# Retention heads on one Trainium2 core: read out at the products, scale later, and pair the rotary columns by partition

## The chip, the cores and the metric

The kernel runs on one core of a Trainium2 chip. The time is device microseconds of one execution. Before the change the median of three runs is 1224.99 us (1224.96 to 1226.88). The engines are named as in the profile: PE (TensorE matmul) with PEld (its weight load), DVE (VectorE), ACT (ScalarE), POOL (GpSimd) and SP (the queue that issues most of the DMAs).

## What is computed

Two layers run over a context of 256 tokens and a latent stream of 256 tokens, 1024 wide: first retention with four heads, then a recurrent block, each followed by a gated convolutional feed-forward block. The change lies in the retention layer. Cut to what matters:

```python
q, k, v, g = split(h @ w_in)               # 4 heads; q, k: 256 wide, v, g: 512 wide per head
q, k = rope_2d(q), rope_2d(k * 256**-0.5)  # latent tokens only
y = retention(q, k, v)                     # scores * decay, times v, both directions
out = (silu(g) * groupnorm(y) * gn) @ w_out
# rot inside rope_2d, once by row and once by column of the token grid:
#   x1, x2 = halves;  [x1*cos - x2*sin, x1*sin + x2*cos]
```

The mean in groupnorm is taken out of v beforehand, so that the norm of a head is one factor per token: the reciprocal root of the mean square over the head's 512 channels.

## The kernel before, in words

Channels lie on the partitions, tokens (256 of context, then 256 latent) on the free axis. The weights arrive as 128x128 blocks, eight to a unit of 128x1024, in the order of use that `make_plan` (L96) writes down; 16 blocks make a piece. Each unit is split into a rounded high part `whi` (a copy, on ACT here) and a rest `wlo` (a DVE subtraction, L452), and each activation likewise into `hi` (ACT, L544) and `lo` (DVE, L545). One 128x128 block of a product is therefore three matmuls, high by high, high by low and low by high, L522 to L524 in `mm3`. The third needs `wlo`. `blk` (L506) calls `prep_units` whenever a unit is entered: with a look-ahead of two it issues the `whi` of the unit three ahead on ACT and the `wlo` of the unit two ahead on DVE.

Every engine works through its queue in program order. Side work is put into those queues by `tick` (L357), called once after most products: it issues up to four pending adaLN products, each a multiplication on ACT (L579, `adap`) and an addition on POOL (L580, `ada`); a step of splitting the recurrent block's weights ahead (L471 on ACT, L479 on DVE, results stored by DMA from ACT's queue, `kept`); and up to n deferred functions. `flush` issues all that is deferred.

The loop over heads in `retention` (L1115) runs for head h, where a "product" of q, k or a gate is one unit of weights, 24 matmuls of 512 columns:

- q0, q1, k0, k1: the four column blocks of q and k. Block q0 holds the 128 channels turned by the token's row, 64 x1 above 64 x2, q1 those turned by its column. After each, `tick(2)` and `rope_split` (L893): the context half is split at once, the latent half is turned with `ra` = x cos (L903) and `rb`, built of two operations of 64 partitions each since x1 and x2 are swapped between the halves (L904, L905), then added (L907), and its split is deferred.
- for heads 1 and 2 then the output product of the head before (`ret_out`, four units of weights), and the first gate g0; for head 3 only g0.
- `ret_scores` (three groups of scores times the decay), `ret_v` (four units), gate g1, `ret_av` (weights by v: four PSUM banks `av`, their squares added up on DVE, L992), gate g2, the decay factors of the next head, `ret_stats` (L995: one matmul, a square root on ACT and a reciprocal on DVE, `rstd`, L679), gate g3, and `ret_z` (L1000).

`ret_z` defers five steps. Step c computes `zt` = `av` * gn * `rstd` (L1007, one operand in PSUM), then `zt` * `sg` with the gate's SiLU (L1008, both operands in SBUF), and splits the `zt` of the step before. These steps come out in the ticks of the next head's q and k products, and the four `av` banks stay taken until then. Head 0 has its q, k and two gates from `start`, and its `ret_stats` and `ret_z` are called within head 1, after q0. Head 2's output product is left to the end, after head 3's gates.

Of the kernel before, what the change touches and what calls it, by code (L numbers as in the profile page):

```python
# [8 lines left out]
F32R = mybir.dt.float32r  # L9
AF = mybir.ActivationFunctionType  # L10
ALU = mybir.AluOpType

P = 128
D = 1024
KD = D // P
NT = 512
NS = 256
# [23 lines left out]

CST = {}
NCST = 0
for _n, _w in (("ident", 128), ("sel", 24), ("cos", 512), ("sin", 512), ("dist", 384), ("dpos", 384),
               ("dneg", 384)):
    CST[_n] = (NCST, _w)
    NCST += _w
# [9 lines left out]
def qk_cols(h):  # L57
    return [2 * h, 2 * h + 1, 8 + 2 * h, 8 + 2 * h + 1]
# [37 lines left out]
def make_plan():  # L96
# [4 lines left out]
    def mat(name, ks, cs, kouter=False):  # L101
        ks, cs = list(ks), list(cs)
        blocks.extend((name, k, c) for k in ks for c in cs) if kouter else \
            blocks.extend((name, k, c) for c in cs for k in ks)
# [16 lines left out]
    for h in range(HEADS):  # L121
        if h == 0:
            mat("ret_in", range(KD), qk_cols(0) + [32, 33], True)
            mat("ret_in", range(KD), [34])
        else:
            mat("ret_in", range(KD), qk_cols(h))
            if h < 3:
                out(h - 1)
            mat("ret_in", range(KD), [32 + 4 * h])
        mat("ret_in", range(KD), range(16 + 4 * h, 20 + 4 * h), True)  # L130
        mat("ret_in", range(KD), range(32 + 4 * h + (3 if h == 0 else 1), 36 + 4 * h))
    out(2)
# [164 lines left out]
class Net:  # L297
# [592 lines left out]
                                    self.cc("ident"), ALU.add)  # L890
        self.dd = dd

    def rope_split(self, ps, c):  # L893

        nc = self.nc
        hi = self.slot(dt=F32R, name="qkhi")
        lo = self.slot(dt=F32R, name="qklo")
        a = self.slot([P, NS], name="ra")
        b = self.slot([P, NS], name="rb")
        cos = self.cc("cos", c * NS, NS)  # L900
        sin = self.cc("sin", c * NS, NS)
        nc.scalar.copy(hi[:, :NS], ps[:, :NS])
        nc.vector.tensor_tensor(a, ps[:, NS:], cos, ALU.mult)  # L903
        nc.vector.tensor_tensor(b[0:64], ps[64:128, NS:], sin[64:128], ALU.mult)  # L904
        nc.vector.tensor_tensor(b[64:128], ps[0:64, NS:], sin[0:64], ALU.mult)  # L905
        nc.vector.tensor_tensor(lo[:, :NS], ps[:, :NS], hi[:, :NS].bitcast(F32), ALU.subtract)
        nc.vector.tensor_tensor(a, a, b, ALU.add)  # L907
        self.defer(lambda: self.split(a, hi[:, NS:], lo[:, NS:]))
        return hi, lo

    def ret_scores(self):
        nc = self.nc
# [60 lines left out]
        self.nc.scalar.activation(t, ps, AF.Silu)  # L973
        self.sg.append(t)

    def ret_av(self):
        nc = self.nc
        self.sync()
        self.av, self.avsg = [], self.sg
        acc = None  # L980
        for c in range(4):
            ps = self.ps(name="av")
            for j in range(4):
                self.mm3(ps if j < 2 else ps[:, NS:], [t[:, c * P:(c + 1) * P] for t in self.vs[j]], self.pr[j],
                         j == 0, j == 3)
            self.av.append(ps)
            sq = self.slot(name="gsq")
            nc.scalar.activation(sq, ps, AF.Square)
            if acc is None:
                acc = sq  # L990
            else:
                nc.vector.tensor_tensor(acc, acc, sq, ALU.add)  # L992
        self.gacc = acc

    def ret_stats(self):  # L995
        ps = self.ps(name="gst")
# [3 lines left out]
    def ret_z(self, h):  # L1000

        nc = self.nc
        zs, av, sg, rs = [], self.av, self.avsg, self.grs

        def first(c):
            t = self.slot(name="zt")
            nc.vector.scalar_tensor_tensor(t, av[c], self.pc("gn", 4 * h + c), rs, ALU.mult, ALU.mult)  # L1007
            nc.vector.tensor_tensor(t, t, sg[c], ALU.mult)  # L1008
            hi = self.slot(dt=F32R, name="zhi")
            lo = self.slot(dt=F32R, name="zlo")  # L1010
            return t, hi, lo

        def step(c):
            if c:
                t, hi, lo = prev.pop()
                self.split(t, hi, lo)
                zs.append((hi, lo))
            if c < 4:
                prev.append(first(c))

        prev = []
        self.defer(*[lambda c=c: step(c) for c in range(5)])
        return zs

# [90 lines left out]
    def retention(self):  # L1115
# [5 lines left out]
        zs = None  # L1121
        for h in range(HEADS):
            self.sg = []
            if h == 0:
                qk = [self.rope_split(pss[j], j % 2) for j in range(4)]
                self.silu_g(pss[4])
                self.silu_g(pss[5])
                self.ret_g(h, hl, 2)
                self.decay(0)
            else:  # L1130
                qk = []
                for j, c in enumerate(qk_cols(h)):
                    ps = self.gemm("ret_in", range(KD), c, lambda k: [(0, hl[k])], NT)
                    if h == 1 and j == 0:
                        self.ret_stats()
                        zs = self.ret_z(0)
                    self.tick(2)
                    qk.append(self.rope_split(ps, j % 2))
                self.flush()
                if h < 3:  # L1140
                    self.ret_out(h - 1, zs)
                else:
                    zprev = zs
                self.ret_g(h, hl, 0)
            self.qk = (qk[:2], qk[2:])
            if h == 0:
                self.ret_v(h, hl)
                self.flush()
                self.ret_scores()
                self.ret_g(h, hl, 3)  # L1150
                self.ret_av()
                self.decay(1)
            else:
                self.flush()
                self.ret_scores()
                self.ret_v(h, hl)
                self.ret_g(h, hl, 1)
                self.ret_av()
                self.ret_g(h, hl, 2)
                if h < 3:  # L1160
                    self.decay(h + 1)
            if h:
                self.ret_stats()
                self.ret_g(h, hl, 3)
                zs = self.ret_z(h)
        self.ret_out(2, zprev)
        self.flush()
        self.need("f0")
# [493 lines left out]
def shape_constants():  # L1662
# [7 lines left out]
    def put(name, a):  # L1670
        o, w = CST[name]
        cst[:, o:o + w] = a

    cos, sin = [], []
    for pos in (t // GRID_W, t % GRID_W):
        ang = freqs[:, None] * pos.astype(np.float32)[None, :]
        cos.append(np.concatenate([np.cos(ang), np.cos(ang)], 0))
        sin.append(np.concatenate([np.sin(ang), -np.sin(ang)], 0))
    put("cos", np.concatenate(cos, 1))
    put("sin", np.concatenate(sin, 1))  # L1680
    dist = np.arange(384)[None, :] - 128.0 - np.arange(P)[:, None]
    put("dist", dist)
    put("dpos", np.maximum(dist, 0))
# [9 lines left out]
def pack(inputs):  # L1693
# [7 lines left out]
    for l in range(2):  # L1701
        mats[f"up{l}"] = a["ffn_w_up"][l]
        mats[f"down{l}"] = a["ffn_w_down"][l]
    order = np.array(lru_order())
    both = np.concatenate([order, W + order])
    mats["lru_in"] = mats["lru_in"][:, both]
# [84 lines left out]
```

## Time and profile before

| What | Before |
|---|---|
| median of three runs | 1224.99 us |
| the profiled execution's own time | 1223.15 us |
| its span, first to last instruction | 1221.4 us |
| PE busy | 1186.3 us (97%) |
| DVE busy | 892.5 us (73%) |
| ACT busy | 731.9 us (60%) |
| POOL busy | 360.0 us (29%) |
| mean granted PE clock | 0.988 |

The profiled execution took 1.8 us less than the median of the three runs, and its span leaves out 1.75 us around the first and last instruction. A share of busy time is an average over stages: where PE is busy 97% of the span, the rest lies in few places, and they are found with the list of PE's waits and the timeline. [...]

### The profile page before, as it was taken

To read this page: it belongs to the slowest core of one execution; us is meant where nothing else is said; L and a number is where in the kernel's file an instruction comes from. 1 tells how busy PE (TensorE), PEld (TensorE's weight loads), DVE (VectorE), ACT (ScalarE), POOL (GpSimd) and SP (SyncE) were. 2 spreads that over 40 slices of the span, in tenths; PEclk is the share of its full clock that TensorE was granted. 3 is DMA by queue.
4 is the path that set the end of the run, shared out by engine and by line. 5 is a ranking of instruction groups with operands and counts; after the bars stand their busy time and mean duration, and the time that the engine had idled before them with its cause. 6 is when DMAs were issued, how large, how long until landed. Compare 5 with 4: busy or idle time off the path is not lost.

```text
span 1221.4 us, 18028 instructions
## 1 busy us (share of the span) xinstructions
PE 1186.3 (97%) x6768; PEld 1010.2 (83%) x6768; DVE 892.5 (73%) x1285; ACT 731.9 (60%) x1100; POOL 360.0 (29%) x238
## 2 busy tenths in 40 slices
PE   9999799999979999999999999999999999999997
PEld 5678688778868889877878888789988788999996
DVE  5665996896596598599945676754658877988743
ACT  5465566765753545987643656542497956666542
POOL 0000555746370012798733435360000001000010
PEclk9999899999989999999999999999999999999999
DMA  9975479758566482445688645654586994655631
GB/s 334 339 253 216 182 238 318 250 193 310 208 224 212 145 319 100 143 154 191 215 313 268 222 153 203 231 196 159 162 313 204 327 333 162 193 187 183 195 107 35
DMA packets 79160, 265.38 MB, mean 217 GB/s; under 512 B 9312, under 2 KB 13024, under 8 KB 79072
## 3 DMA queue, kind: packets, MB, share of 16 engines
q1 hardware_dynamic: 66976, 221.75, 54.0%
q10 hardware_dynamic: 12096, 42.47, 8.9%
q8 instruction: 53, 0.87, 0.3%
q14 instruction: 35, 0.29, 0.1%
HBM read 219.62 MB, written 42.99 MB: 215 GB/s over the span
## 4 chain that ended last, share of the span: by engine, by line
PE 78%; DVE 12%; ACT 3%; DMA 3%; issue 2%; SPq 1%; DVEq 0%; ACTq 0%
PE ps L522 22%; PE ps L524 22%; PE ps L523 22%; DVE wlo L452 3%; PE ps L946 2%; PE ps L947 2%; PE ps L948 2%; DVE rstd L679 1%; ACT adap L579 1%; DVE fzlo L545 1%; PE av L524 1%; PE av L523 1%; PE av L522 1%; DVE zt L1007 1%; PE ps L1639 1%
## 5 line engine op out<-in xcount | busy, mean ns | idle before, releaser
L580 POOL TENSOR_TENSOR ada<-ada,adap 128x512 f32<-128x512 f32 x196 | 324.2, 1679 | 365.5 <-ACT adap L579 232.4
L524 PE MATMUL ps<-hhi,wlo 128*128 128x512 f32 (+1 forms) x640 | 245.6, 384 | 11.2 <-DVE wlo L452 11.2
L522 PE MATMUL ps<-hhi,whi 128*128 128x512 f32 (+1 forms) x640 | 248.7, 389 | 0.0
L523 PE MATMUL ps<-hlo,whi 128*128 128x512 f32 (+1 forms) x640 | 244.2, 382 | 0.0
L665 POOL TENSOR_TENSOR sq<-sq,sq 128x256 f32<-128x256 f32 x29 | 32.4, 1127 | 472.9 <-ACT sq L659 382.9
L523 PE MATMUL ps<-hx,whi 128*128 128x256 f32 x592 | 168.1, 284 | 0.4 <-DVE hx L698 0.2
L522 PE MATMUL ps<-hx,whi 128*128 128x256 f32 x592 | 168.3, 284 | 0.2 <-ACT hx L697 0.2
L524 PE MATMUL ps<-hx,wlo 128*128 128x256 f32 x592 | 167.5, 283 | 0.0
L524 PEld LDWEIGHTS ps<-hhi,wlo 128*128 128x128 f32 x640 | 121.6, 190 | 37.4 <-DVE wlo L452 14.5
L522 PEld LDWEIGHTS ps<-hhi,whi 128*128 128x128 f32 x640 | 121.7, 190 | 31.6 <-issue 6.5
L523 PEld LDWEIGHTS ps<-hlo,whi 128*128 128x128 f32 x640 | 121.7, 190 | 22.9 <-issue 1.0
L522 PEld LDWEIGHTS ps<-hx,whi 128*128 128x128 f32 x592 | 113.5, 192 | 4.2 <-issue 2.5
L523 PEld LDWEIGHTS ps<-hx,whi 128*128 128x128 f32 x592 | 113.5, 192 | 1.2 <-DVE hx L698 0.8
L524 PEld LDWEIGHTS ps<-hx,wlo 128*128 128x128 f32 x592 | 113.5, 192 | 0.0
L1190 DVE SCALAR_TENSOR_TENSOR cv<-ps,par,cv 128x510 f32<-128x510 f32 (+1 forms) x88 | 53.9, 613 | 61.7 <-ACT cv L1187 61.7
L1187 ACT ACTIVATE cv<-ps,par 128x512 f32<-128x512 f32 (+1 forms) x88 | 58.7, 670 | 65.8 <-PE ps L524 64.9
L522 PE MATMUL ps<-fzhi,whi 128*128 128x512 f32 (+1 forms) x198 | 72.7, 367 | 0.0
L524 PE MATMUL ps<-fzhi,wlo 128*128 128x512 f32 (+1 forms) x198 | 72.4, 365 | 0.0
L523 PE MATMUL ps<-fzlo,whi 128*128 128x512 f32 (+1 forms) x198 | 72.4, 365 | 0.0
L708 DVE SCALAR_TENSOR_TENSOR xc<-ps,mod,xc 128x256 f32<-128x256 f32 x48 | 23.0, 479 | 54.5 <-PE ps L524 54.4
L524 PE MATMUL ps<-zhi,wlo 128*128 128x512 f32 (+1 forms) x152 | 55.7, 366 | 7.4 <-DVE wlo L452 7.4
L1191 DVE SCALAR_TENSOR_TENSOR cv<-ps,par,cv 128x510 f32<-128x510 f32 (+1 forms) x88 | 54.2, 616 | 3.1
(791 smaller groups left out, 2786.4 us busy)
## 6 DMA issues: line engine op xcount, KB each, us to landing
kept<-pre ACTq DMA_DIRECT2D x40, 512.0 KB, 5.7
whi<-kept SPq DMA_DIRECT2D x40, 512.0 KB, 4.3
wlo<-kept SPq DMA_DIRECT2D x40, 512.0 KB, 5.5
ak<-wpk SPq DMA_DIRECT2D x32, 256.0 KB, 6.3
xc<-xt SPq DMA_DIRECT2D x4, 256.0 KB, 3.7
x<-xt SPq DMA_DIRECT2D x4, 256.0 KB, 5.2
xst<-xhi SPq DMA_DIRECT2D x16, 64.0 KB, 3.8
cst<-cst SPq DMA_DIRECT2D x3, 192.0 KB, 5.1
```

Of the source, the lines that this page charges most:

```text
L452: self.eng(e).tensor_tensor(d[q, o:n], r[q, o:n], hi[q, o:n].bitcast(F32), ALU.subtract)
L522: mm(ps, w[0], x[0], start=start, stop=False)
L523: mm(ps, w[0], x[1], start=False, stop=False)
L524: mm(ps, w[1], x[0], start=False, stop=stop)
L580: nc.gpsimd.tensor_tensor(acc[i, s], acc[i, s], t, ALU.add)
L665: nc.gpsimd.tensor_tensor(self.acc[s], self.acc[s], sq, ALU.add)
L946: mm(pss[t], xh, wh, start=k == 0, stop=False)
L947: mm(pss[t], xh, wl, start=False, stop=False)
L948: mm(pss[t], xl, wh, start=False, stop=k == KD - 1)
L1187: nc.scalar.activation(acc, ps[:, :n], AF.Identity, scale=w(1), bias=self.pc("fcb", layer * 44 + f))
L1190: nc.vector.scalar_tensor_tensor(a3[:, :, 1:], p3[:, :, :NS - 1], w(0), a3[:, :, 1:], ALU.mult, ALU.add)
L1191: nc.vector.scalar_tensor_tensor(a3[:, :, :NS - 1], p3[:, :, 1:], w(2), a3[:, :, :NS - 1], ALU.mult, ALU.add)
```

## The change

Four edits go together.

1. `rope_split`: the columns of q and k are laid out anew when the weights are packed, so that a block holds all x1 (rows' 64, then columns' 64) and the next block their partners x2. Turning a pair takes a cosine product and a sine product of 128 partitions for each block, and then one subtraction and one addition. Both splits are deferred after the second block. The cosine and sine tables are half as wide.
2. `readout`: `av` * gn * `sg` is computed as soon as the product and its gate exist (all four in `ret_av` for head 0; for heads 1 to 3 two in `ret_av`, one after g2, one after g3). `ret_z` then multiplies by `rstd` and splits.
3. In heads 1 and 2 the gate g0 moves between q1 and k0, with its `tick`; the plan of the weights follows.
4. Head 2's `ret_z` moves from the end of head 2 to behind head 3's scores.

```diff
         else:
-            mat("ret_in", range(KD), qk_cols(h))
+            q, g = qk_cols(h), [32 + 4 * h]
+            mat("ret_in", range(KD), q[:2] + g + q[2:] if h < 3 else q + g)
             if h < 3:
                 out(h - 1)
-            mat("ret_in", range(KD), [32 + 4 * h])
...
-    def rope_split(self, ps, c):
+    def rope_split(self, ps, first=None):
...
         nc.scalar.copy(hi[:, :NS], ps[:, :NS])
-        nc.vector.tensor_tensor(a, ps[:, NS:], cos, ALU.mult)
-        nc.vector.tensor_tensor(b[0:64], ps[64:128, NS:], sin[64:128], ALU.mult)
-        nc.vector.tensor_tensor(b[64:128], ps[0:64, NS:], sin[0:64], ALU.mult)
+        nc.vector.tensor_tensor(a, ps[:, NS:], self.cc("cos"), ALU.mult)
+        nc.vector.tensor_tensor(b, ps[:, NS:], self.cc("sin"), ALU.mult)
         nc.vector.tensor_tensor(lo[:, :NS], ps[:, :NS], hi[:, :NS].bitcast(F32), ALU.subtract)
-        nc.vector.tensor_tensor(a, a, b, ALU.add)
-        self.defer(lambda: self.split(a, hi[:, NS:], lo[:, NS:]))
-        return hi, lo
+        if first:
+            hi0, lo0, a0, b0 = first
+            nc.vector.tensor_tensor(a0, a0, b, ALU.subtract)
+            nc.vector.tensor_tensor(b0, b0, a, ALU.add)
+            self.defer(lambda: self.split(a0, hi0[:, NS:], lo0[:, NS:]), lambda: self.split(b0, hi[:, NS:], lo[:, NS:]))
+        return hi, lo, a, b
...
                 nc.vector.tensor_tensor(acc, acc, sq, ALU.add)
+            self.readout(h)
         self.gacc = acc
+
+    def readout(self, h):
+
+        c = len(self.zt)
+        if c < min(len(self.av), len(self.sg)):
+            t = self.slot(name="zt")
+            self.nc.vector.scalar_tensor_tensor(t, self.av[c], self.pc("gn", 4 * h + c), self.sg[c], ALU.mult, ALU.mult)
+            self.zt.append(t)
...
         def step(c):
             if c:
-                t, hi, lo = prev.pop()
-                self.split(t, hi, lo)
+                hi = self.slot(dt=F32R, name="zhi")
+                lo = self.slot(dt=F32R, name="zlo")
+                self.split(zt[c - 1], hi, lo)
                 zs.append((hi, lo))
             if c < 4:
-                prev.append(first(c))
+                nc.vector.tensor_tensor(zt[c], zt[c], rs, ALU.mult)
...
-                    qk.append(self.rope_split(ps, j % 2))
+                    qk.append(self.rope_split(ps, qk[-1] if j % 2 else None))
+                    if j == 1 and h < 3:
+                        self.ret_g(h, hl, 0)
                 self.flush()
                 if h < 3:
                     self.ret_out(h - 1, zs)
                 else:
-                    zprev = zs
-                self.ret_g(h, hl, 0)
+                    self.ret_g(h, hl, 0)
...
                 self.flush()
                 self.ret_scores()
+                if h == 3:
+                    zprev = self.ret_z(2)
                 self.ret_v(h, hl)
                 self.ret_g(h, hl, 1)
-                self.ret_av()
+                self.ret_av(h)
                 self.ret_g(h, hl, 2)
+                self.readout(h)
...
                 self.ret_g(h, hl, 3)
-                zs = self.ret_z(h)
+                self.readout(h)
+                if h != 2:
+                    zs = self.ret_z(h)
```

## Rows read from the trace of the kernel before

**Rows 1.** PE's waits, whole span: us in total, times, longest us.

```profile
PE ps L524 <- DVE wlo L452: 18.5, 9, 6.0
```

**Rows 2.** PE's timeline, head 1: start, duration, line, tiles, idle time before.

```profile
137.92 0.39 PE L522 MATMUL ps<-zhi,whi 128*128 128x512 f32 x1
138.14 0.39 PE L523 MATMUL ps<-zlo,whi 128*128 128x512 f32 x1
144.56 0.79 PE L524 MATMUL ps<-zhi,wlo 128*128 128x512 f32 x1 [6.03 <-DVE wlo L452]
...
151.18 0.40 PE L522 MATMUL ps<-zhi,whi 128*128 128x512 f32 x1
```

**Rows 3.** The same, heads 2 and 3.

```profile
244.36 0.39 PE L522 MATMUL ps<-hhi,whi 128*128 128x512 f32 x1
...
252.66 0.39 PE L522 MATMUL ps<-zhi,whi 128*128 128x512 f32 x1
...
343.03 0.39 PE L522 MATMUL ps<-hhi,whi 128*128 128x512 f32 x1
...
348.47 0.39 PE L522 MATMUL ps<-hhi,whi 128*128 128x512 f32 x1
...
352.10 0.80 PE L524 MATMUL ps<-hhi,wlo 128*128 128x512 f32 x1 [3.01 <-DVE wlo L452]
...
363.43 0.80 PE L524 MATMUL ps<-hhi,wlo 128*128 128x512 f32 x1 [4.03 <-DVE wlo L452]
...
371.26 0.39 PE L522 MATMUL ps<-qkhi,qkhi 128*128 128x512 f32 x1
```

**Rows 4.** Stretches: us, then PE, PEld, DVE, ACT, POOL busy, granted clock, DMA share, GB/s.

```profile
137.92:174.63 36.71, 30.68 (x121) 24.33 (x120) 36.30 (x54) 24.38 (x38) 28.62 (x18) 0.86 0.61 208
227.90:250.38 22.48, 22.24 (x101) 18.06 (x97) 21.95 (x24) 14.28 (x24) 13.90 (x8) 1.00 0.75 258
331.70:375.41 43.71, 36.67 (x148) 29.48 (x146) 42.01 (x50) 25.87 (x42) 22.89 (x14) 0.88 0.55 184
```

**Rows 5.** DVE's timeline, head 1.

```profile
114.64 0.69 DVE L992 TENSOR_TENSOR gsq<-gsq,gsq 128x512 f32<-128x512 f32 x1 [1.41 <-ACT gsq L988]
...
122.40 3.35 DVE L679 RECIPROCAL rstd<-sd 128x512 f32<-128x512 f32 x1 [2.10 <-ACT sd L677]
...
130.40 0.42 DVE L905 TENSOR_TENSOR rb<-ps,cst 64x256 f32<-64x256 f32 x1
130.84 0.42 DVE L906 TENSOR_TENSOR qklo<-ps,qkhi 128x256 fp32r<-128x256 f32 x1
131.19 0.42 DVE L907 TENSOR_TENSOR ra<-ra,rb 128x256 f32<-128x256 f32 x1
131.52 1.22 DVE L452 TENSOR_TENSOR wlo<-raw22b,whi 128x1024 fp32r<-128x1024 f32 x1
...
134.36 2.31 DVE L479 TENSOR_TENSOR raw21b<-raw21b,pre 128x1024 fp32r<-128x1024 f32 x1
...
142.22 2.28 DVE L452 TENSOR_TENSOR wlo<-raw24a,whi 128x1024 fp32r<-128x1024 f32 x1
```

**Rows 6.** The tiles' operations, all heads: ns min/median/max of each, first and last start.

```profile
L1007 DVE SCALAR_TENSOR_TENSOR zt<-av,par,rstd x16: 737/742/751, 126.8 to 440.8; 128x512 f32<-128x512 f32 x16
L1008 DVE TENSOR_TENSOR zt<-zt,sg x16: 691/693/1484, 127.5 to 441.6; 128x512 f32<-128x512 f32 x16
L907 DVE TENSOR_TENSOR ra<-ra,rb x16: 415/416/1108, 63.8 to 371.0; 128x256 f32<-128x256 f32 x16
```

**Rows 7.** POOL's timeline, head 1.

```profile
132.02 3.57 POOL L580 TENSOR_TENSOR ada<-ada,adap 128x512 f32<-128x512 f32 x2 [129.75 <-PE adat L613]
140.75 13.18 POOL L580 TENSOR_TENSOR ada<-ada,adap 128x512 f32<-128x512 f32 x8 [5.17 <-ACT adap L579]
```

**Rows 8.** DVE's timeline, end of head 2 and `ret_v` of head 3.

```profile
329.07 0.42 DVE L888 TENSOR_TENSOR decay<-decay,dx 128x256 f32<-128x256 f32 x1 [5.07 <-ACT decay L882]
...
395.36 0.69 DVE L954 TENSOR_REDUCE vm<-ps 128x1 f32<-128x512 f32 x1 [10.54 <-PE ps L948]
```

More of the change, by code (lines that the diff above doesn't have):

```diff
@@ L43 @@
 NCST = 0
-for _n, _w in (("ident", 128), ("sel", 24), ("cos", 512), ("sin", 512), ("dist", 384), ("dpos", 384),
+for _n, _w in (("ident", 128), ("sel", 24), ("cos", 256), ("sin", 256), ("dist", 384), ("dpos", 384),
                ("dneg", 384)):
@@ L899, in rope_split @@
         b = self.slot([P, NS], name="rb")
-        cos = self.cc("cos", c * NS, NS)
-        sin = self.cc("sin", c * NS, NS)
         nc.scalar.copy(hi[:, :NS], ps[:, :NS])
-        nc.vector.tensor_tensor(a, ps[:, NS:], cos, ALU.mult)
-        nc.vector.tensor_tensor(b[0:64], ps[64:128, NS:], sin[64:128], ALU.mult)
-        nc.vector.tensor_tensor(b[64:128], ps[0:64, NS:], sin[0:64], ALU.mult)
+        nc.vector.tensor_tensor(a, ps[:, NS:], self.cc("cos"), ALU.mult)
+        nc.vector.tensor_tensor(b, ps[:, NS:], self.cc("sin"), ALU.mult)
         nc.vector.tensor_tensor(lo[:, :NS], ps[:, :NS], hi[:, :NS].bitcast(F32), ALU.subtract)
-        nc.vector.tensor_tensor(a, a, b, ALU.add)
-        self.defer(lambda: self.split(a, hi[:, NS:], lo[:, NS:]))
-        return hi, lo
+        if first:
[4 more added lines that the diff above has]
+        return hi, lo, a, b
     def ret_scores(self):
@@ L974, in silu_g, with ret_av @@
         self.sg.append(t)
-    def ret_av(self):
+    def ret_av(self, h):
         nc = self.nc
         self.sync()
-        self.av, self.avsg = [], self.sg
+        self.av, self.zt = [], []
         acc = None
@@ L1002, in ret_z @@
         nc = self.nc
[L1003 to L1011, printed above, removed]
+        zs, zt, rs = [], self.zt, self.grs
         def step(c):
             if c:
-                t, hi, lo = prev.pop()
-                self.split(t, hi, lo)
+                hi = self.slot(dt=F32R, name="zhi")
+                lo = self.slot(dt=F32R, name="zlo")
+                self.split(zt[c - 1], hi, lo)
                 zs.append((hi, lo))
             if c < 4:
-                prev.append(first(c))
-        prev = []
+                nc.vector.tensor_tensor(zt[c], zt[c], rs, ALU.mult)
         self.defer(*[lambda c=c: step(c) for c in range(5)])
@@ L1123, in retention @@
             self.sg = []
+            qk = []
             if h == 0:
-                qk = [self.rope_split(pss[j], j % 2) for j in range(4)]
+                for j in range(4):
+                    qk.append(self.rope_split(pss[j], qk[-1] if j % 2 else None))
                 self.silu_g(pss[4])
@@ L1130, in retention @@
             else:
-                qk = []
                 for j, c in enumerate(qk_cols(h)):
@@ L1142, in retention @@
                 else:
-                    zprev = zs
-                self.ret_g(h, hl, 0)
+                    self.ret_g(h, hl, 0)
+            qk = [t[:2] for t in qk]
             self.qk = (qk[:2], qk[2:])
@@ L1155, in retention @@
                 self.ret_scores()
+                if h == 3:
+                    zprev = self.ret_z(2)
                 self.ret_v(h, hl)
                 self.ret_g(h, hl, 1)
-                self.ret_av()
+                self.ret_av(h)
                 self.ret_g(h, hl, 2)
+                self.readout(h)
                 if h < 3:
@@ L1676, in shape_constants @@
         ang = freqs[:, None] * pos.astype(np.float32)[None, :]
[L1677 to L1680, printed above, removed]
+        cos.append(np.cos(ang))
+        sin.append(np.sin(ang))
+    put("cos", np.concatenate(cos, 0))
+    put("sin", np.concatenate(sin, 0))
     dist = np.arange(384)[None, :] - 128.0 - np.arange(P)[:, None]
@@ L1703, in pack @@
         mats[f"down{l}"] = a["ffn_w_down"][l]
+    qk = np.arange(2 * D).reshape(2 * HEADS, 2, 2, 64).transpose(0, 2, 1, 3).reshape(-1)
+    mats["ret_in"] = np.concatenate([mats["ret_in"][:, qk], mats["ret_in"][:, 2 * D:]], 1)
     order = np.array(lru_order())
```

## The prediction, written before the changed kernel was run

> **What bounds the kernel now.** I read the page first: PE is busy 97% of the span, so a gain can only come from the rest or from slow matmuls. The list of PE's waits says what the rest is: nine waits of 18.5 us together for a `wlo` that DVE had not finished [rows 1]. The timeline of PE places the longest in heads 1 and 3 of the retention layer, and shorter ones in head 2. At full clock a product's 24 matmuls take 5.44 us, 0.227 us each (343.03 to 348.47) [rows 3]. In head 1, PE stands 6.03 us at the first block of `ret_out`. It then goes on at half speed: from 137.92 to 151.18 there are 18 matmuls, worth 4.1 us, so 9.2 us are lost [rows 2]. In head 2, 27 matmuls (6.1 us) lie between 244.36 and 252.66: 2.2 us lost. In head 3, 48 matmuls (10.9 us) lie between 348.47 and 371.26, with waits of 3.01 and 4.03 us: 11.9 us lost [rows 3]. Together 23.3 us. The granted clock of these stretches is 0.86, 1.00 and 0.88 [rows 4], so a wait of 3 us or more is paid about 1.6 times: 9.2 for 6.03, 11.9 for 7.04. [...]
>
> Why `wlo` is late: in these stretches DVE is busy 36.3 of 36.7 us, 22.0 of 22.5 and 42.0 of 43.7 [rows 4]. It holds `rstd`, the whole of `ret_z`, four ropes, the weights split ahead and the units' own `wlo`, in one queue. What matters is how much DVE work lies between `rstd` and the `wlo` that PE needs, and how much PE work lies beside it.
>
> DVE's price for one operation has two values. With one operand in PSUM, `zt` of L1007 takes 0.74 us always; with both in SBUF, L1008 takes from 0.69 to 1.48 us and L907 from 0.42 to 1.11 [rows 6]. A `wlo` takes 1.22 us before POOL begins to add, a split ahead 2.31 us and a `wlo` 2.28 us while it adds [rows 5, 7].
>
> **The change part by part.**
>
> *Readout.* In head 0 the four L1007, 4 x 0.74 = 3.0 us, leave the crowded stretch for `ret_av`, where DVE idles between the squares (1.41 us before each) [rows 5], so they cost nothing there; without that idle time they would cost their 3.0 us. In heads 1 to 3 two run in `ret_av`, one waits for the SiLU of g2, one for that of g3. Behind the first wait stand the decay and `rstd`; before the decay DVE waits 5.07 us for ACT anyway [rows 8], so this is free unless the exponentials slip. The one after g3 stays in the stretch: 0.74 us in heads 1 and 2. The later product with `rstd` replaces the one with `sg`, at the same price, so nothing is saved there. PSUM banks come free sooner, but no wait of PE names a bank, so I count nothing.
>
> *Rotary layout.* Four half-partition operations become two full ones per pair: two operations of 0.43 us (start to start 0.44) go [rows 5], 0.9 us a pair, 1.7 us a head. Both splits now wait for the second block; for q that is covered by g0 or k, for k by `ret_out` in heads 1 and 2. In head 3 only g0's 5.44 us cover it. The smaller tables save 256 KB of transfer, at which nothing waits: zero.
>
> *First gate.* PE gets 5.44 us more work before `ret_out`. DVE gets one more `wlo` (1.2 to 2.3 us) before it, and the gate's tick brings four adaLN products forward, so POOL's eight adds (13.18 us from 140.75 on [rows 7]) begin earlier, by at most the 5.44 us of a product, beside the operations that the next `wlo` waits for. ACT gets a SiLU with its table load earlier, the number of loads unchanged. SP's loads keep their order by position and move with PE.
>
> *Head 2's scaling behind head 3's scores.* Head 3's stretch loses 4 L1007, 4 L1008 and 4 `zlo`; one L1007 comes back at g3. `ret_v` gets them instead (without L1007, 4 x 1.4 = 5.5 us), where DVE idles 10.54 us [rows 8]: free as long as `ret_v`'s units are split in time; otherwise at most 5.5 us.
>
> **The sum.**
>
> Head 1, walking DVE's queue from 122.40 to k1's `wlo` (raw24a; with g0 in front that unit is k1's): `rstd` 3.35; split ahead 1.2; two products 1.3; rope of q0, three operations 1.3; `wlo` 1.2; `zlo`, of the form of L1008, 0.7; then, while POOL adds, split ahead 2.3, product 1.0, `zlo` 1.0; product 0.7; rope of q1 1.3, its two sums between 0.42 and 1.11, 1.9; `wlo` 2.3. The durations make 19.6 us; neighbours overlap by 0.07 us (131.19 against 130.84 + 0.42) [rows 5], twelve times 0.8: 18.8, so it is ready at 141.2. PE reaches it at the same place as now, 138.14 + 0.23 = 138.4 [rows 2]. The wait becomes 2.8 us in place of 6.03, paid at 1.6: 4.5 us. Gain 9.2 - 4.5 = 4.7. Bounds: 9.2 if the sums and `wlo` run at the low price (1.1 + 1.1 us less) and ACT is in time; zero if ACT's turns keep DVE waiting 3 us.
>
> Head 2: DVE's queue loses three L1007 (2.2 us) and 0.9 us of rope, and PE gets 5.44 us of work against one `wlo` of at most 2.3. That is 6.2 us more room where 2.2 were lost; POOL's earlier adds take part of it. Gain 2.0, bounds 0 and 2.2.
>
> Head 3: DVE fills its stretch, 42.0 of 43.7 us [rows 4], so what leaves its queue brings the scores forward. Out go four L1007 (3.0), four L1008 and four `zlo` of the same form, about 1.05 each between 0.69 and 1.48 [rows 6] (8.4), and 1.7 of rope, 13.1 us; in comes 0.74: 12.4, against 11.9 that PE lost. But the last `wlo`, two sums and four `qklo`, which now run when POOL is done, then fall beside its 14 adds (22.89 us [rows 4]): up to 1.1 + 6 x 0.7 = 5.3 us more, and I take half, 2.6. About 2 us of the wait stay: gain 10. Bounds 5 (all of it, and paid at 1.6) and 11.9.
>
> Sum: 4.7 + 2.0 + 10 = 16.7 us. The profiled execution took 1223.15 us, 1.84 below the median, so 1206.4 for its like; against the median of 1224.99 I predict **1208.3 us**.
>
> [...] Steps from L905 to L906 and on are 0.44 and 0.35 us [rows 5]. [...]
>
> What the readout takes away reads PSUM, and what stays reads two SBUF tensors. [...]
>
> **The rivals.**
>
> *All waits go.* If DVE stays just ahead in all three heads, all 23.3 us come back: 1201.7. For it: in heads 2 and 3 it is near. Against: head 1's walk ends 2.8 us late with POOL's adds at the high price.
>
> *The wait moves.* `wlo` of k1 in head 1 and of g0, or the last `qklo`, in head 3 are late in place of the old ones. Head 1 gains 0 to 1, head 2 gains 1, head 3 gains 5: 1218. For it: POOL's adds come earlier, and ACT, which feeds them, does not get lighter.
>
> *The change does not reach the path.* The edits take 4.7 us from head 1's queue but give POOL's adds a tick, ACT a SiLU, DVE a `wlo`. If ACT's copies are what DVE waits for, heads 1 and 2 lose what head 3 gains: 1224 to 1226.
>
> *Slower.* One mechanism: POOL's adds start with head 1's `rstd` rather than at 132.02 [rows 7] and run on without a break through heads 1 and 2. With every operation on two SBUF tensors at its highest, the walk of head 1 gets 6.7 us on top (split ahead 1.1, `wlo` 1.1, six of the form of L1008 4.2, sums 0.3): a wait of 9.5 us, paid 15, 6 more than now. Head 2 the same way loses 6 in place of 2.2, and with head 3 gaining 6 the sum is 4 us slower: 1229. It decides once the adds begin before about 126. Against: the first adds need the products that q1's tick issues, and the change does not move that tick.
>
> **How the numbers follow.** Forecast 0.55 (1204 to 1213), all waits go 0.17 (1200 to 1204), the wait moves 0.18 (1213 to 1222), not on the path 0.06, slower 0.04. A measurement can tell about 0.2%, 2.4 us, from no change. So faster 0.91 (the first three, and a little of the fourth), same 0.05, slower 0.04. The range 1201 to 1218 takes in the forecast, most of the first rival and half of the second, 0.8.
>
> **What would show it.** Right: PE's waits at `ret_out` of head 1 and in head 3's k1 and g0 are gone or under 1.5 us; a wait of 2 to 3 us stands at head 1's k1; the readout takes 0.74 us in `ret_av` beside idle time; DVE's idle time in head 3's `ret_v` falls by about 5.5 us; the spans of the other stages stay. Wrong: waits for `wlo` of over 12 us together in the retention layer, waits on the readout's SiLU that reach `rstd`, or a change in the feed-forward or recurrent stages.

## The result, and the profile after

The changed kernel takes 1209.99 us (median of four, 1208.33 to 1211.38) beside 1224.97 for the kernel before on the same chip: ratio 0.9877, 95% interval 0.9857 to 0.9897, 15 us less. Predicted were 1208.3 us in a range of 1201 to 1218. The profiled execution took 1208.33 us with a span of 1206.6 us, 14.8 less than before.

From the page and from the list of PE's waits (us in total, times, longest), after:

```profile
PE 1180.6 (98%) x6768; PEld 1006.3 (83%) x6768; DVE 888.3 (74%) x1269; ACT 731.3 (61%) x1100; POOL 364.5 (30%) x238
...
PE ps L524 <- DVE wlo L452: 7.0, 4, 3.1
```

The wait that was 18.5 us in nine pieces [rows 1] is 7.0 in four. The busy times of PE, DVE and ACT change by under 1%: the change moves work, it hardly saves any. The fourth `wlo` wait, 2.29 us, lies in the feed-forward block, where before had one of 2.31.

PE's timeline after (start, duration, line, tiles, idle time before). The `av` rows are the first products of `ret_av` in heads 1, 2 and 3; up to each of them PE has had the same number of matmuls in both kernels (946, 1420 and 1790).

```profile
141.12 0.50 PE L524 MATMUL ps<-hhi,wlo 128*128 128x512 f32 x1 [3.13 <-DVE wlo L452]
...
199.63 0.39 PE L522 MATMUL av<-phi,vhi 128*128 128x512 f32 x1
...
229.06 0.50 PE L524 MATMUL ps<-hhi,wlo 128*128 128x512 f32 x1 [1.34 <-DVE wlo L452]
...
272.44 1.06 PE L594 MATMUL ada<-ada,onehot 128*32 128x512 f32 x6
274.12 1.05 PE L594 MATMUL ada<-ada,onehot 128*32 128x512 f32 x2 [0.61 <-POOL ada L580]
...
306.61 0.39 PE L522 MATMUL av<-phi,vhi 128*128 128x512 f32 x1
...
349.45 0.50 PE L524 MATMUL ps<-hhi,wlo 128*128 128x512 f32 x1 [0.21 <-DVE wlo L452]
...
387.71 0.39 PE L522 MATMUL av<-phi,vhi 128*128 128x512 f32 x1
...
445.02 0.59 PE L669 MATMUL st<-sq,ones_d 128*128 128x256 f32 x2
```

The same `av` rows and the last one, which begins the next block, in the kernel before:

```profile
206.01 0.39 PE L522 MATMUL av<-phi,vhi 128*128 128x512 f32 x1
...
311.82 0.39 PE L522 MATMUL av<-phi,vhi 128*128 128x512 f32 x1
...
403.86 0.39 PE L522 MATMUL av<-phi,vhi 128*128 128x512 f32 x1
...
461.22 0.70 PE L669 MATMUL st<-sq,ones_d 128*128 128x256 f32 x2
```

Subtracting gives the gain by head: 6.38 us by head 1's `av` (206.01 - 199.63), 5.21 by head 2's, 16.15 by head 3's. So head 1 gained 6.4, head 2 gave back 1.2, and head 3 gained 10.9. At the end of the layer 16.2 us are gained; the rest of the kernel takes 761.6 us where it took 760.2, which leaves the span's 14.8.

DVE's timeline after: the readout in `ret_av`, the second rope pair of head 1 with what follows it, and `ret_v` of head 3.

```profile
110.99 0.74 DVE L1001 SCALAR_TENSOR_TENSOR zt<-av,par,sg 128x512 f32<-128x512 f32 x1
112.48 0.69 DVE L992 TENSOR_TENSOR gsq<-gsq,gsq 128x512 f32<-128x512 f32 x1 [0.74 <-ACT gsq L988]
...
130.31 1.22 DVE L479 TENSOR_TENSOR raw21b<-raw21b,pre 128x1024 fp32r<-128x1024 f32 x1
131.45 1.77 DVE L1021 TENSOR_TENSOR zt<-zt,rstd 128x512 f32<-128x512 f32 x1
133.14 1.79 DVE L545 TENSOR_TENSOR zlo<-zt,zhi 128x512 fp32r<-128x512 f32 x1
...
135.46 0.41 DVE L901 TENSOR_TENSOR ra<-ps,cst 128x256 f32<-128x256 f32 x1
135.79 0.41 DVE L902 TENSOR_TENSOR rb<-ps,cst 128x256 f32<-128x256 f32 x1
...
136.45 0.99 DVE L906 TENSOR_TENSOR ra<-ra,rb 128x256 f32<-128x256 f32 x1
137.36 1.50 DVE L907 TENSOR_TENSOR rb<-rb,ra 128x256 f32<-128x256 f32 x1
138.78 2.28 DVE L452 TENSOR_TENSOR wlo<-raw24a,whi 128x1024 fp32r<-128x1024 f32 x1
...
379.20 0.69 DVE L954 TENSOR_REDUCE vm<-ps 128x1 f32<-128x512 f32 x1 [5.02 <-PE ps L948]
```

The readout takes 0.74 us, with idle time still left behind it where [rows 5] had 1.41. k1's `wlo` ends at 138.78 + 2.28 = 141.06; predicted was 141.2. The rope's steps are 0.33 us, not 0.44 [rows 5]. Head 3's `ret_v` keeps 5.02 us of the 10.54 idle [rows 8]: the scaling went there and no wait of PE follows it.

### The profile page after: what moved, and what is told of

Read it like the earlier page. It is cut to its first block, busy times and chain, and to the rows that moved or that the text cites. A ratio compares the mean times of both kernels' runs of the same rounds, so it can differ in the third digit from the quotient of the medians.

```text
span 1206.6 us, 18016 instructions
## 1 busy us (share of the span) xinstructions
PE 1180.6 (98%) x6768; PEld 1006.3 (83%) x6768; DVE 888.3 (74%) x1269; ACT 731.3 (61%) x1100; POOL 364.5 (30%) x238
## 4 chain that ended last, share of the span: by engine, by line
PE 73%; DVE 11%; ACT 7%; issue 4%; DMA 3%; POOL 1%; SPq 1%; ACTq 0%; DVEq 0%; POOLq 0%
PE ps L522 21%; PE ps L524 20%; PE ps L523 20%; DVE wlo L452 2%; ACT adap L579 2%; PE ps L946 2%; PE ps L948 2%; PE ps L947 2%; ACT whi L420 1%; DVE zlo L545 1%; PE av L523 1%; PE av L522 1%; PE av L524 1%; PE ps L1648 1%; POOL ada L580 1%
## 5 line engine op out<-in xcount | busy, mean ns | idle before, releaser
L580 POOL TENSOR_TENSOR ada<-ada,adap 128x512 f32<-128x512 f32 x196 | 328.9, 1704 | 353.4 <-ACT adap L579 350.1
L708 DVE SCALAR_TENSOR_TENSOR xc<-ps,mod,xc 128x256 f32<-128x256 f32 x48 | 23.0, 478 | 56.0 <-PE ps L524 55.9
L522 PE MATMUL ps<-zhi,whi 128*128 128x512 f32 (+1 forms) x152 | 54.4, 358 | 0.0
```

The lines of the kernel that those rows point to most:

```text
L522: mm(ps, w[0], x[0], start=start, stop=False)
L580: nc.gpsimd.tensor_tensor(acc[i, s], acc[i, s], t, ALU.add)
```

## The experiments

"The changed kernel" below is the one just shown, 1209.99 us. The kernel before, timed beside them, had medians of 1225.2 (runs 1 to 4), 1225.55 (5 to 8) and 1223.9 us (9, 10 and the second profile of run 4).

**1. The gate behind `ret_out` again.**

```diff
-            mat("ret_in", range(KD), q[:2] + g + q[2:] if h < 3 else q + g)
+            mat("ret_in", range(KD), qk_cols(h))
...
+            mat("ret_in", range(KD), [32 + 4 * h])
...
-                    if j == 1 and h < 3:
-                        self.ret_g(h, hl, 0)
...
-                else:
-                    self.ret_g(h, hl, 0)
+                self.ret_g(h, hl, 0)
```

> The changed kernel with g0 of heads 1 and 2 back behind the output product; all else as changed. My theory (DVE's queue up to the weights and activations that PE needs next, with POOL's adds doubling its two-SBUF operations): in head 1 the wlo of the unit after k0 comes in time or under 1.5 us late, since the gate's tick no longer pulls POOL's adds forward, but the output product begins 5.4 us earlier and finds its third and fourth zlo unfinished: waits for zlo or wlo of 4 to 6 us together at the head of ret_out in head 1, against 3.1 us now, and 0.5 to 2 us in head 2. Time 1211 to 1215 us, 1 to 5 us over the changed kernel's 1210. Rival (the gate brings nothing, since it moves as much DVE and POOL work forward as PE work): waits in head 1 of 2.5 to 3.5 us, time 1209 to 1211.

Measured: 1207.08 us (1205.49 to 1208.82), ratio 0.9859, 0.9843 to 0.9875. Not slower: the theory missed, and of the rival the wait came but not the time, which is 2 us under its range. PE's timeline, head 1:

```profile
141.00 0.50 PE L524 MATMUL ps<-zhi,wlo 128*128 128x512 f32 x1 [3.13 <-DVE wlo L452]
```

The wait is as long as in the changed kernel, 3.13 us, only now at `ret_out`'s first block: the unit in that place of the order (raw24a) is late, whichever product it belongs to. The extra gate only puts k's unit there instead of `ret_out`'s; no PE work comes to stand in front of the late `wlo`. The waits for `zlo` behind it are 0.5 us together, not the 4 to 6 us expected. POOL's second group of adds begins at 135.74, against 135.86 with the gate in front, so the gate does not bring its start forward either; with it the group holds twelve adds in place of eight. Edit 3 brought nothing. Of the 2.9 us that this kernel is shorter, only 1.0 lies in the retention layer (its end at 444.00 for 445.02).

**2. Head 2's scaling back at the end of head 2.**

```diff
-                if h == 3:
-                    zprev = self.ret_z(2)
...
-                if h != 2:
+                if h == 2:
+                    zprev = self.ret_z(2)
+                else:
                     zs = self.ret_z(h)
```

> The changed kernel with head 2's ret_z back at the end of head 2, so its four products and splits come out in head 3's ticks; all else as changed. Theory: DVE's queue in head 3 gets four products and four zlo back, 8 times 0.7 to 1.0 us with POOL adding, some 8 us, against almost no wait now (0.2 us): waits for wlo of 5 to 7 us in head 3, and with PE at half clock after the longer ones a time of 1217 to 1221 us, 7 to 11 over the changed kernel. Rival (the readout and the new rope alone already clear head 3, which stood within 12 us of being clear): waits of under 2 us, time 1210 to 1212.

Measured: 1218.72 us (1216.43 to 1220.23), ratio 0.9952, 0.9936 to 0.9968; 8.7 us over the changed kernel. PE's timeline in head 3:

```profile
344.92 0.50 PE L524 MATMUL ps<-hhi,wlo 128*128 128x512 f32 x1 [1.40 <-DVE wlo L452]
...
356.76 0.79 PE L524 MATMUL ps<-hhi,wlo 128*128 128x512 f32 x1 [6.10 <-DVE wlo L452]
```

The first wait is followed at a granted clock of 1.00, the second at 0.50 for 5 us. Head 3's waits are back, as the theory said, and most of head 3's gain belongs to this edit: from head 2's `av` to head 3's it takes 90.5 us, in the changed kernel 81.1.

**3. The readout of heads 0 and 1 back in `ret_z`.**

```diff
-        if c < min(len(self.av), len(self.sg)):
+        if h >= 2 and c < min(len(self.av), len(self.sg)):
...
-            if c < 4:
+            if c < 4 and h < 2:
+                t = self.slot(name="zt")
+                nc.vector.scalar_tensor_tensor(t, av[c], self.pc("gn", 4 * h + c), rs, ALU.mult, ALU.mult)
+                nc.vector.tensor_tensor(t, t, sg[c], ALU.mult)
+                zt.append(t)
+            elif c < 4:
                 nc.vector.tensor_tensor(zt[c], zt[c], rs, ALU.mult)
```

> The changed kernel with the readout of heads 0 and 1 back behind the norm: their zt is made from av in the ticks of the next head's q and k, as before, and the av banks stay taken until then; heads 2 and 3 as changed. Theory: DVE's queue in head 1 gets 4 x 0.74 us back, two of them ahead of k1's wlo, the other two as well: the wait there grows from 3.1 to 5.5 to 6.5 us and is followed by half clock; in head 2 three are added (2.2 us) after the wait at q1 and lead to 0 to 2 us more. Time 1213 to 1217, 3 to 7 us over the changed kernel. Rival (the early readout matters through the freed banks or not at all): if through banks, PE waits that name DVE zt or av appear; if not at all, time 1209 to 1211.

Measured: 1214.51 us (1212.84 to 1216.66), ratio 0.9923, 0.9904 to 0.9943. PE, POOL and ACT in head 1, then the same row of ACT in the changed kernel:

```profile
145.07 0.80 PE L524 MATMUL ps<-hhi,wlo 128*128 128x512 f32 x1 [6.14 <-DVE wlo L452]
...
139.85 19.91 POOL L580 TENSOR_TENSOR ada<-ada,adap 128x512 f32<-128x512 f32 x12 [3.24 <-ACT adap L579]
...
137.25 0.62 ACT L544 CAST zhi<-zt 128x512 fp32r<-128x512 f32 x1 [3.31 <-DVE zt L1023]
```

```profile
133.25 0.62 ACT L544 CAST zhi<-zt 128x512 fp32r<-128x512 f32 x1 [1.80 <-DVE zt L1021]
```

The wait doubles, 3.13 to 6.14, and no wait names a PSUM bank: the readout's worth is the length of DVE's queue. The POOL row also says where its adds' start is set. In the changed kernel they begin 4.0 us earlier, at 135.86, because ACT's multiplications for POOL stand in ACT's queue behind a copy that waits for DVE's `zt`, and this copy begins 4.0 us earlier too; a shorter DVE queue releases ACT, and so POOL, sooner.

**4. The old rotary layout.**

```diff
-        nc.vector.tensor_tensor(b, ps[:, NS:], self.cc("sin"), ALU.mult)
+        nc.vector.tensor_tensor(b[0:64], ps[64:128, NS:], sin[64:128], ALU.mult)
+        nc.vector.tensor_tensor(b[64:128], ps[0:64, NS:], sin[0:64], ALU.mult)
...
+        nc.vector.tensor_tensor(a, a, b, ALU.add)
+        self.defer(lambda: self.split(a, hi[:, NS:], lo[:, NS:]))
```

> The changed kernel with the rotary layout of before (a cosine product, two half-partition sine products and a sum for each block, split deferred after each); all else as changed. Theory: DVE's cost ahead of k1's wlo in head 1 hardly differs: by the traces the old rope takes 1.99 us start to start, 4.0 for the pair with one sum late, the new one 1.0 for q0 and 3.3 for q1, since both sums fall beside POOL's adds, 4.3 for the pair. So the wait of 3.1 us stays within 1 us, and heads 2 and 3, which have room, show waits under 1.5 us: time 1208 to 1212, no difference that three rounds can tell. Rival (count of operations: two of 0.43 us less a pair are time gained): 0.9 us in head 1 ahead of k1's wlo, 1.7 us in heads 2 and 3 where DVE is the limit, time 1212 to 1215.

Measured: 1217.81 us (1212.41 to 1221.79, six executions), ratio 0.9942, 0.9919 to 0.9965. This is above both expectations. The profile fell on the shortest. DVE, then PE, in head 3:

```profile
353.93 0.41 DVE L903 TENSOR_TENSOR ra<-ps,cst 128x256 f32<-128x256 f32 x1
...
355.58 1.12 DVE L907 TENSOR_TENSOR ra<-ra,rb 128x256 f32<-128x256 f32 x1
...
362.06 0.50 PE L524 MATMUL ps<-qkhi,qklo 128*128 128x512 f32 x1 [1.16 <-DVE qklo L906]
```

A block takes 1.65 us up to its sum (353.93 to 355.58); in the changed kernel 0.99 (135.46 to 136.45). That is 0.66 a block, 2.6 us a head where 1.7 was counted, and in head 3, with no `ret_out` between k and the scores, PE waits for it: 1.16 us at the row shown and 1.07 just before.

*The same kernel profiled in another execution*, to see why its executions spread:

> The same kernel as in the run rope_back, for a second profile. That run's profile fell on its shortest execution, 1212.4 us, where its others lay between 1216 and 1222. If a wait of 3 to 4 us is sometimes followed by half clock and sometimes not, a longer execution shows the same waits as the first profile (3.8 us in head 1, 3 us in head 3) with stretches of half clock behind them. If it is another cause, the waits themselves are longer or at other places.

It took 1219.28 us, 6.9 over the first profile. PE's timeline, then a row of ACT's:

```profile
141.68 0.79 PE L524 MATMUL ps<-hhi,wlo 128*128 128x512 f32 x1 [3.77 <-DVE wlo L452]
...
233.64 0.50 PE L524 MATMUL ps<-hhi,wlo 128*128 128x512 f32 x1 [3.01 <-DVE wlo L452]
...
207.80 1.05 ACT L420 CAST whi<-raw38a 128x1024 fp32r<-128x1024 f32 x1 [7.66 <-DMA raw38a<-wpk]
```

The first wait was 3.76 us in the other profile; behind it the granted clock was 0.66 there and is 0.50 here, over 5 us. The second wait is new: `rstd` of head 1 begins at 228.34 here and at 224.34 in the other profile, with the same DMA share of 0.94 from 185 to 215 us. Most of these 4.0 us are there at the ACT row: the same `whi` begins at 204.63 in the other profile. Its load leaves SP's queue at 202.04 here and at 198.02 there, here after a wait of 7.2 us for a store of weights split ahead (`kept<-raw32a`). Run 6 is about this place. Both waits differ between executions of one program.

**5. POOL's adds kept out of the q, gate and k ticks of heads 1 to 3** (`ada_rate` is how many adaLN products a tick issues; they follow later).

```diff
             else:
+                self.ada_rate = 0
                 for j, c in enumerate(qk_cols(h)):
...
                 self.flush()
+                self.ada_rate = 4
```

> The changed kernel with no adaLN products issued in the ticks of q, g0 and k of heads 1 to 3; they come out in the ticks behind, four each as before. Nothing is computed otherwise. Theory (POOL's adds double DVE's two-SBUF operations, and that is what is left of head 1's wait): ahead of k1's wlo the rows of the changed kernel show 1.77, 1.79, 0.99, 1.50 and 2.28 us where the low prices are 0.69, 0.69, 0.41, 0.41 and 1.22, 4.9 us more: without them the wait of 3.13 us in head 1 is gone, and these operations show their low prices. Of the 3.1 us head 2 keeps some or gives some back at q1, where rstd is late. Time 1206 to 1209 us. Rival (ACT's turns or the number of DVE operations set it): the wait of head 1 stays over 2 us, time 1209 to 1211.

Measured: 1204.98 us (1204.34 to 1207.64), ratio 0.9839, 0.9818 to 0.986. DVE, then PE:

```profile
134.11 0.69 DVE L545 TENSOR_TENSOR zlo<-zt,zhi 128x512 fp32r<-128x512 f32 x1
...
136.64 0.42 DVE L907 TENSOR_TENSOR rb<-rb,ra 128x256 f32<-128x256 f32 x1
136.97 1.22 DVE L452 TENSOR_TENSOR wlo<-raw24a,whi 128x1024 fp32r<-128x1024 f32 x1
...
174.19 0.47 PE L946 MATMUL ps<-whi,hhi 128*128 128x512 f32 x1 [1.18 <-DVE x L708]
```

Without POOL beside it (the first add begins at 142.24), `zlo` takes 0.69 us in place of 1.79, the sum 0.42 in place of 1.50, `wlo` 1.22 in place of 2.28. Head 1's wait is gone. The edit takes ACT's multiplications for POOL out of this stretch as well, but from `rstd` to the end of this `wlo` DVE takes 14.6 us in place of 19.5, and the 4.9 us between them are the lower prices of five operations, two of the form of `zlo`, two sums and `wlo`. So POOL's adds set what was left of the wait; behind them small waits take its place (`ret_out`'s residuals at L708, `vlo`).

**6. Two pieces of the weights that are split ahead moved far behind** (208 and 224 to 848 and 880).

```diff
-PRE = (80, 96, 112, 176, 192, 208, 224, 304, 320, 336, 352, 416, 432, 448, 464, 720, 752, 784, 944, 976)
+PRE = (80, 96, 112, 176, 192, 304, 320, 336, 352, 416, 432, 448, 464, 720, 752, 784, 848, 880, 944, 976)
```

> The changed kernel with two of the twenty pieces of the recurrent block's weights, which are loaded, split and stored ahead during head 1's ret_v and gates, moved to the feed-forward block; nothing is computed otherwise. Theory (in head 1's ret_av and gates the transfers are at their limit, over 400 GB/s and 99% busy between 190 and 210 us: ACT's whi waits for its load, the squares of av and with them rstd come late, and PE waits 1.34 us at q1 of head 2, which takes back what head 1 had gained): the squares follow av within 1 us, rstd comes 2 to 6 us earlier against its matmul, and the wait at q1 of head 2 is gone. Head 1's wait of 3.1 us stays. Time 1207 to 1209. Rival (rstd is late since the readouts wait for the gates' SiLU in DVE's queue ahead of the decay): the wait at q1 of head 2 stays within 0.5 us of 1.34, time 1209 to 1212.

Measured: 1207.98 us (1204.71 to 1208.23), ratio 0.9859, 0.9838 to 0.9881. The stretch of head 1's `ret_av` (us, then PE, PEld, DVE, ACT, POOL busy, granted clock, DMA share, GB/s) in this kernel:

```profile
185.00:215.00 30.00, 30.00 (x145) 25.23 (x144) 19.09 (x23) 16.49 (x24) 14.85 (x10) 1.00 0.68 237
```

and in the changed kernel, with rows of its ACT and DVE timelines:

```profile
185.00:215.00 30.00, 29.61 (x141) 24.44 (x140) 22.49 (x26) 20.01 (x30) 15.35 (x10) 1.00 0.90 332
...
201.50 1.18 ACTq L488 DMA_DIRECT2D kept<-raw34b  x1
202.78 1.05 ACT L420 CAST whi<-raw38a 128x1024 fp32r<-128x1024 f32 x1 [5.53 <-PE av L524]
...
215.37 2.31 DVE L479 TENSOR_TENSOR raw37a<-raw37a,pre 128x1024 fp32r<-128x1024 f32 x1
...
220.95 0.72 ACT L887 ACTIVATE decay<-dexp 128x256 f32<-128x256 f32 x2 [2.65 <-DVE dexp L876]
```

Head 2's wait at 229.06 is gone. In the changed kernel ACT stands 5.53 us before one `whi`, with the gate's SiLU and the squares of `av` queued behind it. But this kernel also reaches `ret_av` 2.2 us later, which alone would cover a wait of 1.34. What tells the two apart is `rstd` against the products before it, over all runs. The last column counts from the last row of `ret_stats`' product on PE to `rstd` on DVE:

| Kernel | DMA share, 185 to 215 | `ret_av` begins | `rstd` begins | between | from `ret_stats`' product |
|---|---|---|---|---|---|
| before | 0.91 | 206.01 | 228.18 | 22.2 | 7.25 |
| changed | 0.90 | 199.63 | 223.71 | 24.1 | 9.16 |
| run 1 | 0.87 | 201.73 | 224.00 | 22.3 | 7.36 |
| run 2 | 0.93 | 199.75 | 223.48 | 23.7 | 8.83 |
| run 3 | 0.94 | 204.74 | 226.27 | 21.5 | 6.63 |
| run 4 | 0.94 | 202.32 | 224.34 | 22.0 | 7.09 |
| run 4, second profile | 0.94 | 202.52 | 228.34 | 25.8 | 10.90 |
| run 5 | 0.94 | 199.45 | 223.51 | 24.1 | 8.42 |
| run 6 | 0.68 | 201.84 | 222.53 | 20.7 | 6.41 |
| run 7 | 0.69 | 197.24 | 217.93 | 20.7 | 6.41 |
| run 8 | 0.72 | 196.38 | 217.68 | 21.3 | 6.40 |
| run 9 | 0.79 | 200.57 | 224.25 | 23.7 | 6.41 |
| run 10 | 0.78 | 197.62 | 221.33 | 23.7 | 6.41 |

With the two pieces moved (runs 6 to 10), `rstd` follows the product of `ret_stats` by 6.4 us in every kernel, however early that is; the 23.7 us of runs 9 and 10 hold two waits of PE for `vlo` before that product. With the pieces in their place it takes 6.6 to 10.9 us, and `rstd` comes no sooner than 223.5. So there the split ahead of these pieces sets it, and part of what PE gained in head 1 is lost.

Whether its transfers or its operations do so was not separated, since the edit takes both away. The expectation named the load of the `whi`, with over 400 GB/s from 190 to 210 us; the window shows 349 GB/s in the mean, at a share of 0.93, and no limit of the transfers is shown. In run 4's second profile ACT does stand until that load lands. In the changed kernel it issues four stores of split weights before the `whi`, the last until 202.68, and later the decay factors wait 2.65 us for DVE's `dexp`, which is queued behind the split of `raw37a`.

**7. Both side edits, 5 and 6, on the changed kernel.**

> The two edits together on the changed kernel. Theory: they act at different places, so the waits in heads 1 and 2 are both gone, nothing is given back, and the gains add up: 4.5 to 6 us, 1204 to 1206 us. Rival (the transfers or another queue take back whatever is won): no better than the better of the two alone.

Measured: 1204.76 us (1204.43 to 1207.81), ratio 0.9845, 0.9823 to 0.9866. The long waits of heads 1 and 2 are both gone; with POOL's adds moved but the two pieces in place (run 5), 0.61 us still stood in head 2's q1. The time is in the expected range, yet no better than run 5 alone (1204.98), as the rival said: the 5.0 and 2.0 us of runs 5 and 6 do not add up. Waits in `ret_v` and `ret_av` take their place (under run 8).

**8. Both side edits on run 1** (gate behind `ret_out`).

> The kernel with the gate back behind the output product, with both edits. Theory: without POOL's adds DVE's queue up to the first output block in head 1 shrinks by the same 4.9 us and the wait of 3.13 us there goes, with at most 1 us left for a zlo; head 2 had no wait. Time 1203 to 1205, 2 to 4 us under that kernel's 1207, and within 2 us of the same edits with the gate in front: where DVE is in time, the gate's place is worth nothing. Rival (the gate's 5.4 us of PE work are needed as cover): 2 to 4 us slower than with the gate in front.

Measured: **1201.62 us** (1200.76 to 1205.66), ratio 0.982, 0.9795 to 0.9844: the shortest median of the study, 3.1 us under run 7, where the theory expected at most 2 us of difference and the rival a slower kernel; the two intervals meet. PE's waits from 130 us to 462 us:

```profile
PE st L671 <- ACT sq L659: 0.8, 1, 0.8
PE av L524 <- DVE vlo L962: 0.4, 1, 0.4
```

Run 7 in the same stretch, besides these two kinds (0.8 and 1.1 us there):

```profile
PE ps L946 <- DVE x L708: 3.1, 2, 1.9
```

With the gate in front, `ret_out` stands right before the scores, and `ret_v`'s first product waits for its residuals (`x`, L708); with the gate between them it does not. The layer ends at 437.29 here and at 441.17 in run 7.

**9. Both side edits on the kernel before**: how much of the gain is POOL and transfers alone?

> The kernel before the change, with the two side edits alone: no adaLN products in the ticks of q and k of heads 1 to 3, and two pieces of the recurrent block's weights prepared later. None of the change's four edits. Theory (POOL's adds beside DVE's two-SBUF operations make up as much of the old waits as the operations that the change removes): in head 1 the rows of before hold 3.5 us of extra price ahead of the first output block's wlo, so the wait of 6.03 falls to about 2.5 us; in head 3 they hold some 8 us, against waits of 7.04, which fall to under 1 us; 2 to 3 us come back as waits at ret_v, where the adds then run. Time 1207 to 1212 us, about that of the changed kernel. Rival (the count of DVE operations decides, POOL only adds a little): waits in heads 1 and 3 of over 8 us together, time 1216 to 1222.

Measured: 1218.67 us (1215.77 to 1219.95), ratio 0.9945, 0.9923 to 0.9968. PE's timeline:

```profile
141.50 0.50 PE L524 MATMUL ps<-zhi,wlo 128*128 128x512 f32 x1 [2.51 <-DVE wlo L452]
...
360.43 0.50 PE L523 MATMUL ps<-qklo,qkhi 128*128 128x512 f32 x1 [2.02 <-DVE qklo L545]
```

Head 1's wait is what the theory said, 2.51 us. Head 3's are 4.1 us together (1.30, 2.02 and 0.78) where under 1 was expected, 3.7 us for `vlo` come on top, and the time is the rival's, though these waits are 6.6 us where it named over 8: the old DVE queue is too long even at the low prices. The layer ends at 453.71, 7.5 us earlier than in the kernel before without them (461.22), and 16.4 later than in run 8, which has edits 1, 2 and 4 as well. Without the side edits, edits 1, 2 and 4 bring 17.2 us there (444.00 in run 1). So the side edits alone do not give what the change gives, and with them its edits are worth about as much as without.

**10. Run 8 with the old rotary layout.**

> The kernel with the gate back and both side edits (1201.6 us), with the rotary layout of before. Theory: DVE is in time everywhere there, so 2.4 us a head more of DVE work (old pair 4.0 us start to start, new one 2.7) stays under cover in heads 1 and 2; in head 3, where g0 alone covers k's rope, the scores may wait up to 1.5 us. Time 1201 to 1204. Rival (the old layout costs by itself, wherever, as its run on the changed kernel says): 1206 to 1210.

Measured: 1205.21 us (1203.70 to 1208.86), ratio 0.9841, 0.9806 to 0.9876; 3.6 us over run 8, between the two expectations, and the intervals meet. PE's timeline:

```profile
199.39 0.50 PE L524 MATMUL av<-phi,vlo 128*128 128x512 f32 x1 [1.16 <-DVE vlo L962]
```

The longer queue is paid even where nothing else is late: its backlog reaches `vlo` in `ret_v`, two more such waits of 1.18 and 0.88 us follow, and the layer ends 4.8 us later than in run 8 (442.11).

## Why the prediction was right, and which steps were not

The main mechanism was right, and the total as near as it is because its errors cancelled, which is luck: 4.7, 2.0 and 10 us were predicted for heads 1, 2 and 3, and 6.4, -1.2 and 10.9 came; 16.7 against 16.2 at the layer's end, of which 1.4 was lost later.

- *What bounds the kernel* held: `wlo` behind a full DVE queue. Undoing one edit at a time costs 8.7 us (scaling), 7.8 (layout), 4.5 (readout) and -2.9 (gate). The four add to 18.1, over the 15.0 gained. That would fit edits that share one queue, but with the layout's six executions 9 us apart the difference is not shown.
- *Head 1.* The walk of DVE's queue held to 0.14 us (141.06 for 141.2), though its terms did not: `L1021` and `zlo` took 1.77 and 1.79, priced at 1.0; the split ahead 1.22, priced at 2.3. The wait was 3.13 us for 2.8. Its price, "paid at 1.6", did not come: behind this wait the granted clock stayed at 1.00, and the gain was 6.4. That is one execution's luck. In run 6 the same wait of 3.13 us was followed by 0.66; counted from head 0's `av` (105.44 before, 105.37 and 106.23) head 1 then gains 5.0 us and not 6.3, and 4.7 were predicted.
- *Head 2* failed: "POOL's earlier adds take part of it" left out `rstd`. `ret_av` came 6.4 us earlier, `rstd` only 4.5 (the table of run 6), and PE waited 1.34 us. Then PE waited for a sum of POOL's: 272.44 to the scores at 275.09 is 2.65 us for eight products that take 1.07 elsewhere. The two cost 2.9 us, more than the 2.2 there were to win.
- *Head 3* held: `ret_v` took the scaling free (5.02 us idle left, 5.5 fewer, as said), and 0.21 us of the waits stayed where 2 us were expected.
- *Layout* was mis-sized: 0.9 us a pair, measured 1.3 (run 4). I had taken the old step of 0.44 for every operation; the full-width ones step at 0.33. The rows show 0.44 us beside the half-partition operations [rows 5] and 0.33 without them; why they differ was not shown. On run 8 the layout is worth 3.6 us (run 10).
- *The gate* was priced as PE work ahead of the late unit and as the cause of POOL's earlier adds. Run 1 shows neither. The adds begin earlier because DVE's shorter queue releases ACT (run 3).
- *The second rival*, that the wait moves because POOL's adds come earlier, describes what was left of head 1's wait: run 5 removes it. The rows put the price of POOL beside DVE at up to 1.1 us for each operation on two SBUF operands, 128x256 (0.42 to 1.50) as for 128x1024 (1.22 to 2.28).

**Open.** Why the same wait is followed by one clock or the other, and why the store that held the load of `raw38a` in run 4's second profile was later than in the first, was not settled. That the gate costs 2.9 us rests on kernels timed at different times, and its interval meets the changed kernel's; run 8 against run 7, timed together, gives 3.1, and there too the intervals meet.

## What to carry to other kernels

Where the bound is a queue rather than an engine's sum, move work out of the stretch in which that queue is late into a stretch where it idles; what counts is the count of instructions ahead of the one that is waited for, each at the price it has beside its neighbours. Then ask whom the shorter queue releases: here ACT, through it POOL, and POOL's adds raised the price of the operations beside them (`zlo` from 0.69 us to 1.79, `wlo` from 1.22 to 2.28). A lead won in one stage is kept only if the side work of the next stage, here the loads, copies and stores of weights split ahead, can follow it: with two of these pieces moved away, `rstd` came 6.4 us after its product, with them in place 6.6 to 10.9.

## What the runs showed of the hardware that was not expected

- One length of wait, two clocks after it. Behind 3.13 us of standstill the granted clock over some 5 us was 1.00 in the changed kernel and in run 2, 0.69 in run 1 and 0.66 in run 6. Behind 3.76 and 3.77 us, in one program, it was 0.66 and 0.50; behind 1.40 us (run 2) it was 1.00.

From the windows of the changed kernel, of run 1 and, with the wait in front, of run 6, the stretch behind the wait (columns as above):

```profile
141.00:146.00 5.00, 4.88 (x21) 4.03 (x22) 5.00 (x8) 4.81 (x9) 5.00 (x3) 1.00 0.31 106
```

```profile
141.00:146.00 5.00, 4.51 (x12) 2.83 (x13) 5.00 (x10) 2.51 (x5) 5.00 (x4) 0.69 0.78 261
```

```profile
141.97 0.50 PE L524 MATMUL ps<-hhi,wlo 128*128 128x512 f32 x1 [3.13 <-DVE wlo L452]
...
142.00:147.00 5.00, 5.00 (x15) 3.96 (x16) 5.00 (x7) 4.66 (x9) 5.00 (x4) 0.66 0.37 112
```

In the first PE does 21 matmuls, in the second 12, in the third 15. A few such places make the spread of 3 to 9 us among a kernel's executions plausible; that was not shown one by one.

- DVE beside POOL: with both operands in SBUF, 128x256 went from 0.42 to 1.50 us, 128x512 from 0.69 to 1.79, 128x1024 from 1.22 to 2.28, up to about 1.1 us on each whatever its size. Beside POOL, operations with one operand in PSUM stayed at 0.74 (the readout, at 231.16 us in the changed kernel) and 0.41 (`ra` at 144.25 in run 1). The surcharge of up to 1.1 us did not grow with the operation, and it lies under the 1.67 us of one of POOL's adds (19.98 us for twelve); by what mechanism the two engines hinder each other was not shown.
